# Attention probabilities of half of the blocks transposed in one TensorE run instead of two

## The chip, the cores and the metric

The kernel runs on one core of a Trainium2 chip. The core has five engines with their own instruction queues: PE (TensorE, the matrix engine, with its weight loads shown apart as PEld), ACT (ScalarE), DVE (VectorE), POOL (GpSimd) and SP (SyncE, which here issues the DMAs). The metric is the device time of one execution in microseconds (us); less is better. The kernel before takes 558.78 us, the median of three runs (558.47 to 558.86).

## The reference, cut to what matters

One encoder layer on a sequence of 512 tokens with 1024 channels, in float32. The normed and modulated input is projected to eight streams of 1024 channels; one branch is a gated recurrence, the other is attention over a grid of 8 rows by 64 columns, and both are projected, merged and normed.

```python
h = rms_norm(x, g_pre[l]) * (1.0 + scl[:, None, :]) + shift[:, None, :]
proj = h @ w_in[l]
xa, za, q, k, v, zb, ga, gb = jnp.split(proj, split_pts, axis=-1)
...
y_b = neighbourhood_attention(qh, kh, vh, rpb[l]) * jax.nn.silu(zb)
y_b = y_b @ w_pb[l]
merged = jax.nn.sigmoid(ga) * y_a + jax.nn.sigmoid(gb) * y_b
x = x + gate[:, None, :] * (merged @ w_o[l])
```

In the attention each of 16 heads lets a query see all 8 rows and a window of 16 columns around its own, with a learned bias per offset and a softmax over the 128 keys:

```python
s = jnp.einsum('bqhd,bwqkhd->bhqwk', q_r, k_win).astype(jnp.float32) * scale
s = s + jnp.transpose(bias, (0, 2, 1, 3)).astype(jnp.float32)[None]
p = jax.nn.softmax(s.reshape(B, H, GRID_W, win_r * WIN_C), axis=-1)
...
return jnp.einsum('bhqwk,bwqkhd->bqhd', p, v_win)
```

## The kernel before, in words

Every float32 product is made of three matmuls of rounded parts (high times high, high times low, low times high), so each operand is split: ACT writes the rounded high part (`whi`, line 380), and DVE or POOL subtracts it for the low part (`wlo`, line 383). A projection (`proj`) takes one 512 KB weight tile and runs 24 matmuls of 128x512 into one PSUM bank named `acc` (three matmuls for each of eight pieces of the contraction, line 386). Some 70 of these projections make up most of the program.

Attention is worked on in four groups of two head pairs. For each group the six projections for q, k and the output gate z come first, then PE computes the scores of both pairs in one piece (`sp`, 48 matmuls). The 64 columns of the grid are cut into four blocks of 16 columns; a block of 128 queries (8 rows by 16 columns) meets 24 or 32 key columns in 8 rows, so 192 keys at the edges (blocks 0 and 3) and 256 inside (blocks 1 and 2). `attend` runs `half` twice for a pair: for the edge blocks and for the inner ones. A half has two tiles of probabilities, each 128 queries by 384 or 512 numbers. For each tile:

- DVE adds the bias to the scores and takes the minimum (`ttr`, line 829); ACT takes the exponential (`exp`, line 836);
- PE transposes the tile in pieces of 128x128 into a bank of class `pt` (`ptr`, line 843): 3 pieces for an edge tile, 4 for an inner one;
- ACT copies the bank rounded to SBUF (`ph`, line 849) and DVE writes the rest beside it (`pl`, line 851), both into a tile `pp`;
- PE multiplies `pp` with the values (`pv`, 4 matmuls of 128x256).

ACT and DVE then put both results of a half together (`ev0`, line 868; `ev1` and `ev2`, lines 871 and 874). After both halves of a pair the sums of the softmax are inverted, go through DRAM to be spread over partitions, and come back as `rcx`; DVE multiplies the gate with them (`szr`, line 899) and then with the attention's result (`yb`, line 901). Both read two operands in SBUF. The tanh part of the next gate is `zt` on ACT (line 882) and `sz` on DVE (line 883).

There are 8 PSUM banks, and a class may hold only so many of them: `LIMITS` gives `pt` two, `pv` two, `acc` three. What runs when is not written by hand: each operation is given to a planner (`Plan`) with an engine, a cost in us and a rank, and the planner commits operations in the order of their ranks as far as their data, an engine and a buffer are free by its own reckoning. Its result is a fixed order of instructions on each engine. The matmuls of projections have ranks that let them fill every place where PE would otherwise wait for an attention step, so the attention's steps lie scattered between them. When an engine reaches an instruction whose inputs aren't there, all that stands behind it on that engine waits too.

Of the kernel before, what the change touches and what calls it, by code (L numbers as in the profile page):

```python
# [334 lines left out]
def layer(ctx, tc, x, x_t, par, w_m, w_v, w_in, w_blk, rpb, amask, w_pa, w_pb, w_o, g_final, out):  # L335
# [8 lines left out]
    def op(eng, cost, fn, rank, name="", **kw):  # L344
        return pl.op(eng, cost, fn, HEAD.get(name, rank), name=name, **kw)
# [18 lines left out]
    def B(cls):  # L364
        return pl.tile(cls, lambda i: ps.tile([P, 512], F32, tag=f"b{i}", name=nm(cls)))
# [31 lines left out]
    def const(name, shape, dt=F32):  # L397
        return pl.fixed(cp.tile(shape, dt, name=name))

    ident, onesc = const("ident", [P, P]), const("onesc", [P, P])  # L400
# [15 lines left out]
       r=[par_sb, ident], w=[pp0])  # L416
# [60 lines left out]
    for i in range(2):  # L477
        st, qs = B("hd"), []
        for j in range(4):
# [4 lines left out]
               r=[xTp[j, i]], w=[q], name=f"sq{i}{j}")  # L484
            if j:
                op(("DVE", "POOL"), (dve(512), pool_(512)), lambda e, a=qs[0], q=q: ENGINE[e].tensor_tensor(a.ap, a.ap, q.ap, op=ALU.add),
                   rank, r=[q], rw=[qs[0]], lock=True, name=f"sqa{i}{j}")
# [28 lines left out]
    for i in range(2):  # L516
        op("ACT", act(256), cast(lambda i=i: rbs.ap[:, 256 * i:256 * i + 256], lambda i=i: rb[i].ap[:, :256]), -1 + 0.4 * i,
           r=[rb[i]], w=[rbs.part()], name=f"rbs{i}")
# [286 lines left out]
    def attend(pr, sps, z, nbt, pos, pos0):  # L805
        sm, yt = C("sm", 8), T("yt")
        off = (pr % 2) * 256

        def half(bs):
            sp = sps[bs[0]]  # L810
            rt = pos0 + 0.1 * bs[0] - 0.2
            spv = lambda h, e: sp[h].ap.rearrange("p (e f) -> p e f", e=2)[:, e, :]
            rk = pos + 0.2 * bs[0]
            nk = nkb[bs[0]]
            edge = bs[0] == 0
            pv = [B("pv"), B("pv")]
            mn = C("mn", 4, 8)

            groups = [[(b, h) for b in bs] for h in range(2)] if edge else [[(b, h) for h in range(2)] for b in bs]
            for members in groups:  # L820
                pt_ = T("p")
                pv2 = lambda i, pt_=pt_: pt_.ap[:, i * nk:(i + 1) * nk]
                for i, (b, h) in enumerate(members):
                    def f(e_, i=i, b=b, h=h, pv2=pv2):
                        v = lambda a: a.rearrange("p (r c) -> p r c", r=ROWS)
                        e = bs.index(b)
                        nb = nbt[(1, 0, 0, 2)[b]].ap.rearrange("p (h f) -> p h f", h=2)
                        o = pv2(i).rearrange("p (c r) -> p r c", r=ROWS)
                        nc.vector.tensor_tensor_reduce(out=o, in0=v(spv(h, e)[:, :nk]), in1=v(nb[:, h, :nk]),  # L829
                                                       scale=1.0, scalar=3e38, op0=ALU.add, op1=ALU.min,  # L830
                                                       accum_out=mn.ap[:, 2 * e + h:2 * e + h + 1])
                    op("DVE", dve(nk) + 0.07, f, rt, r=[sp[h], nbt[(1, 0, 0, 2)[b]]], w=[pt_, mn], name="ttr")
                for i, (b, h) in enumerate(members):
                    def f(e_, i=i, b=b, h=h, pv2=pv2):
                        c = 2 * bs.index(b) + h
                        nc.scalar.activation(pv2(i), pv2(i), AF.Exp, bias=mn.ap[:, c:c + 1], scale=-1.0,  # L836
                                             accum_out=sm.ap[:, 4 * h + b:4 * h + b + 1])
                    op("ACT", act(nk, 1, True), f, rk - 0.25, r=[mn, pt_], w=[pt_, sm], name="exp")
                ptp, nt = B("pt"), nk // 64

                def f(e_, pt_=pt_, ptp=ptp, nt=nt):
                    for j in range(nt):
                        nc.tensor.transpose(ptp.ap[:, j * P:(j + 1) * P], pt_.ap[:, j * P:(j + 1) * P], ident.ap)  # L843
                op("PE", 0.03 + 0.11 * nt, f, rk - 0.3, r=[pt_, ident], w=[ptp], name="ptr")

                pp = W("pp", F32R)
                ppv = lambda pp=pp, nt=nt: pp.ap[:, :nt * 256].rearrange("p (j s q) -> p j s q", j=nt, s=2)
                pv4 = lambda ptp=ptp, nt=nt: ptp.ap[:, :nt * P].rearrange("p (j q) -> p j q", j=nt)
                op("ACT", act(nt * P), lambda e_, ppv=ppv, pv4=pv4: nc.scalar.copy(ppv()[:, :, 0, :], pv4()),  # L849
                   rk - 0.35, r=[ptp], w=[pp], name="ph")  # L850
                op("DVE", dve(nt * P), lambda e_, ppv=ppv, pv4=pv4: nc.vector.tensor_tensor(  # L851
                    ppv()[:, :, 1, :], pv4(), ppv()[:, :, 0, :].bitcast(F32), op=ALU.subtract),
                   rk - 0.35, r=[ptp], rw=[pp], name="pl")

                def f(e_, members=members, ppv=ppv):
                    for i, (b, h) in enumerate(members):
                        e = bs.index(b)
                        for j in range(2):
                            mm(pv[h].ap[:, e * 256:(e + 1) * 256], vt[pr // 2, b, j].ap[:, off + h * P:off + (h + 1) * P],
                               ppv()[:, (i if edge else 2 * i) + j].rearrange("p s q -> p (s q)"), j == 0, j == 1)  # L860
                op("PE", 0.49, f, rk - 0.4, r=[pp] + [vt[pr // 2, b, j] for b in dict(members) for j in range(2)],
                   w=[pv[h] for h in dict((h, b) for b, h in members)], name="pv")

            vp = T("vp")
            p3 = lambda t: t.ap.rearrange("p (e s q) -> p e s q", e=2, s=2)
            v3 = lambda: vp.ap[:, :256].rearrange("p (e q) -> p e q", e=2)
            for h in range(2):
                op("ACT", act(256), lambda e_, h=h: nc.scalar.copy(v3()[H[h]], p3(pv[h])[H[1 - h], :, 0, :]), rk - 0.45,
                   r=[pv[h]], w=[vp], name="ev0")
            for h in range(2):  # L870
                op("DVE", dve(256), lambda e_, h=h: nc.vector.tensor_tensor(v3()[H[h]], p3(pv[h])[H[h], :, 1, :], v3()[H[h]],
                   op=ALU.add), rk - 0.45, r=[pv[h], vp], w=[vp], name="ev1")
            for h in range(2):
                op("DVE", dve(256), lambda e_, h=h: nc.vector.tensor_tensor(
                    yt.ap[H[h]].rearrange("p (b q) -> p b q", b=4)[:, bs[0]:bs[1] + 1:bs[1] - bs[0]], p3(pv[h])[H[h], :, 0, :], v3()[H[h]],
                    op=ALU.add), rk - 0.45, r=[pv[h], vp], w=[yt], name="ev2")
        half((0, 3))
        half((1, 2))

        nz, oz = z  # L880
        sz, rc = T("sz"), rcs[pr % 2]
        op("ACT", act(512), lambda e: nc.scalar.activation(sz.ap, oz.ap, AF.Tanh, scale=0.5), nz - 1.9, r=[oz], w=[sz], name="zt")
        op("DVE", dve(512), lambda e: nc.vector.scalar_tensor_tensor(sz.ap, sz.ap, 1.0, oz.ap, op0=ALU.add, op1=ALU.mult),
           nz - 1.9, r=[oz], rw=[sz], name="sz")

        def recip(e):
            nc.vector.tensor_scalar(rc.ap[:, :8], sm.ap, 2.0, None, op0=ALU.mult)
            nc.vector.reciprocal(rc.ap[:, :8], rc.ap[:, :8])
            nc.vector.transpose(rct.ap[:, :32], rc.ap)


        rct, rcx = T("rct"), T("rcx")
        scr = pl.fixed(dp.tile([32, P], F32, name=f"rscr{pr}"))
        op("DVE", 0.5, recip, pos - 0.3, r=[sm], w=[rc, rct], lock=True, name="rc")
        op("SP", 0.5, lambda e: nc.sync.dma_start(turned(scr.ap), rct.ap[:, :32]), pos - 3, r=[rct], w=[scr], size=16384, late=SLACK, name="rcs")
        for h in range(2):
            src = bass.AP(scr.ap.tensor, scr.ap.offset + h * 512, [[0, 64], [1, 512]])
            load(rcx, lambda h=h: rcx.ap[H[h], :], src, pos - 3, 131072, r=[scr], name="rcl", late=1.0)
        op("DVE", dve(512), lambda e: nc.vector.tensor_tensor(rbc(sz.ap), rbc(sz.ap), nat(rcx.ap), op=ALU.mult),
           pos - 0.3, r=[rcx], rw=[sz], lock=True, name="szr")  # L900
        op("DVE", dve(512), lambda e: nc.vector.tensor_tensor(rbc(sz.ap), nat(yt.ap), rbc(sz.ap), op=ALU.mult), pos + 0.5, r=[yt],
           rw=[sz], lock=True, name="yb")
        ybh[pr], ybl[pr] = two("ybhl")
        op("ACT", act(512), cast(whole(ybh[pr]), whole(sz)), pos + 0.6, r=[sz], w=[ybh[pr]], name="ybh")
        op("DVE", dve(512), sub(whole(ybl[pr]), whole(sz), whole(ybh[pr])), pos + 0.6, r=[sz, ybh[pr]], w=[ybl[pr]], lock=True,
           name="ybl")
# [187 lines left out]
    for k in range(KD):  # L1094
        t, r = W("wc"), gcol.part()
# [51 lines left out]
    for k in range(KD):  # L1147
# [3 lines left out]
        for n in range(2):  # L1151
            v = lambda n=n, raw=raw: raw.ap[:, n * 512:(n + 1) * 512]
            op("DVE", dve(512), lambda e, n=n, v=v: nc.vector.tensor_tensor(v(), v(), gate[n].ap, op=ALU.mult), rank,
               r=[gate[n]], rw=[raw], lock=True, name="wog")
# [165 lines left out]
```

## Time and profile before

| | before |
|---|---|
| median of the runs | 558.78 us (558.47 to 558.86) |
| the profiled execution | 558.32 us |
| its span, first to last instruction | 556.5 us |
| mean granted TensorE clock | 0.996 |
| PE busy | 548.2 us (99%), 2769 matmuls |
| PEld busy | 457.3 us (82%) |
| DVE busy | 395.2 us (71%) |
| ACT busy | 320.6 us (58%) |
| POOL busy | 103.1 us (19%) |

The span is what the trace covers; the execution's own time has 1.8 us around it. The ends of matmuls are modelled and overlap with the next one, so a busy PE says only that a matmul was always in flight. The chain of waits goes back from the last instruction, at each step to what released it; its pieces in a row tell how long PE spent on each piece of work. The timeline shows instructions with their start and length, and idle time ahead of them with what ended it.

### The profile page before, as it was taken

The numbers are of one execution on the slowest core, as the hardware profiler recorded it, in microseconds if no ns is written. First come the engines' busy times: TensorE is split into PE (matmuls) and PEld (weight loads), VectorE is DVE, ScalarE is ACT, GpSimd is POOL, SyncE is SP. The second block draws the span as 40 slices with busy tenths as digits, with TensorE's granted clock in tenths as the row PEclk, the third lists the DMA queues.
The fourth block names the chain that finished last, engine by engine and source line by source line (L and its number), as shares of the span: only waits on it lengthen the run. The fifth ranks groups of instructions, "written<-read, shape, count | busy, mean of one in ns | idle before, by whom it ended". The sixth has DMA issues, their size and how long they took to land.

```text
span 556.5 us, 7644 instructions
## 1 busy us (share of the span) xinstructions
PE 548.2 (99%) x2769; PEld 457.3 (82%) x2769; DVE 395.2 (71%) x707; ACT 320.6 (58%) x557; POOL 103.1 (19%) x98
## 2 busy tenths in 40 slices
PE   8999999999999999999999999999999999999995
PEld 8888888888888888887887888888788888888884
DVE  5998733786786886898449978867968973569423
ACT  6542524863763772775986984996697242223242
POOL 0102657646547430000000000000000000000220
PEclk9999999999999999999999999999999999999998
DMA  8992994851741753035245045132237522480002
GB/s 311 408 407 110 312 296 174 199 166 50 189 145 68 177 146 133 2 102 185 83 145 170 6 146 170 39 114 67 85 104 275 190 77 75 150 304 1 0 38 115
DMA packets 30825, 82.54 MB, mean 148 GB/s; under 512 B 4548, under 2 KB 5700, under 8 KB 30788
## 3 DMA queue, kind: packets, MB, share of 16 engines
q1 hardware_dynamic: 30500, 81.73, 44.4%
q8 instruction: 22, 0.36, 0.3%
q10 hardware_dynamic: 288, 0.33, 0.2%
q14 instruction: 15, 0.12, 0.1%
HBM read 75.60 MB, written 6.44 MB: 147 GB/s over the span
## 4 chain that ended last, share of the span: by engine, by line
PE 99%; DVE 0%; POOL 0%; issue 0%; ACT 0%; POOLq 0%
PE acc L386 79%; PE hx L386 8%; PE pv L386 3%; PE pt L843 2%; PE sp L386 2%; PE gt L386 2%; PE hx L504 1%; PE hx L437 0%; PE hd L551 0%; PE hd L496 0%; PE hd L513 0%; DVE yo L1205 0%; DVE yo L1173 0%; DVE xr L1177 0%; ACT sd L1195 0%
## 5 line engine op out<-in xcount | busy, mean ns | idle before, releaser
L386 PE MATMUL acc<-hhl,whi 128*128 128x512 f32 x784 | 244.6, 393 | 0.0
L386 PEld LDWEIGHTS acc<-hhl,whi 128*128 128x128 f32 x784 | 143.7, 188 | 27.2
L386 PE MATMUL acc<-hhl,wlo 128*128 128x512 f32 x392 | 152.8, 390 | 0.0
L386 PEld LDWEIGHTS acc<-hhl,wlo 128*128 128x128 f32 x392 | 73.6, 188 | 15.8
L380 ACT CAST whi<-wraw 128x1024 fp32r<-128x1024 f32 x72 | 74.3, 1044 | 4.9 <-DMA wraw<-in_w_in_dram 3.7
L1184 POOL TENSOR_TENSOR yo<-yo,gfin 128x512 f32<-128x512 f32 x6 | 8.2, 1360 | 337.1 <-ACT xr L1181 337.1
L383 POOL TENSOR_TENSOR wlo<-wraw,whi 128x1024 fp32r<-128x1024 f32 x23 | 56.4, 2459 | 63.2 <-ACT whi L380 26.4
L383 DVE TENSOR_TENSOR wlo<-wraw,whi 128x1024 fp32r<-128x1024 f32 x49 | 59.3, 1220 | 3.0 <-ACT whi L380 2.8
L386 PE MATMUL acc<-woh,mhl 128*128 128x512 f32 (+1 forms) x144 | 40.4, 365 | 0.0
L386 PE MATMUL acc<-yahl,whi 128*128 128x512 f32 x128 | 39.4, 389 | 0.0
L386 PE MATMUL acc<-ybhl,whi 128*128 128x512 f32 x128 | 39.4, 389 | 0.0
L738 POOL TENSOR_TENSOR nb<-msk,braw 128x192 f32<-128x192 f32 (+1 forms) x48 | 31.1, 682 | 28.5 <-DMA braw<-in_rpb_dram 28.5
L836 ACT ACTIVATE p<-p,mn 128x192 f32<-128x192 f32 (+1 forms) x64 | 30.5, 478 | 5.6 <-DVE mn L829 5.5
L386 PE MATMUL hx<-vh,hhl 128*128 128x512 f32 x112 | 33.5, 389 | 0.0
L1069 DVE SCALAR_TENSOR_TENSOR gm<-gm,acc 128x512 f32<-128x512 f32 x16 | 11.0, 687 | 31.2 <-PE acc L386 31.1
L829 DVE CUSTOM_DVE_ANT_0 p<-sp,nb 128x192 f32<-128x192 f32 (+1 forms) x64 | 31.8, 612 | 0.7 <-POOL nb L738 0.2
L386 PEld LDWEIGHTS acc<-woh,mhl 128*128 128x128 f32 x144 | 26.1, 189 | 4.4
L386 PEld LDWEIGHTS acc<-yahl,whi 128*128 128x128 f32 x128 | 24.0, 188 | 5.0
L386 PEld LDWEIGHTS acc<-ybhl,whi 128*128 128x128 f32 x128 | 24.0, 188 | 5.0
L386 PE MATMUL acc<-wol,mhl 128*128 128x512 f32 (+1 forms) x72 | 26.3, 365 | 0.0
L851 DVE TENSOR_TENSOR pp<-pt,pp 128x384 fp32r<-128x384 f32 (+1 forms) x32 | 19.6, 624 | 8.9 <-ACT pp L849 8.8
L1064 ACT ACTIVATE gm<-acc 128x512 f32<-128x512 f32 x16 | 9.6, 599 | 27.4 <-PE acc L386 27.2
(195 smaller groups left out, 967.3 us busy)
## 6 DMA issues: line engine op xcount, KB each, us to landing
wraw<-in_w_in_dram SPq DMA_DIRECT2D x56, 512.0 KB
wc<-in_w_m_dram SPq DMA_DIRECT2D x22, 512.0 KB
vt<-vscr SPq DMA_DIRECT2D x20, 256.0 KB
vscr<-va SPq DMA_DIRECT2D x8, 512.0 KB
wraw<-in_w_pb_dram SPq DMA_DIRECT2D x8, 512.0 KB
wraw<-in_w_pa_dram SPq DMA_DIRECT2D x8, 512.0 KB
wo<-in_w_o_dram SPq DMA_DIRECT2D x8, 512.0 KB
wv<-in_w_v_dram SPq DMA_DIRECT2D x7, 512.0 KB
```

Of the source, the lines that this page charges most:

```text
L380: return lambda e: nc.scalar.copy(o(), i()) if e == "ACT" else nc.vector.tensor_copy(o(), i())
L383: return lambda e: ENGINE[e].tensor_tensor(o(), a(), b().bitcast(F32), op=ALU.subtract)
L386: nc.tensor.matmul(o, a, b, start=first, stop=last)
L504: op("PE", 0.3, lambda e: nc.tensor.matmul(wb.ap[:, :P], onesc.ap, onesc.ap, start=True, stop=True), 5000 + j, r=[onesc], hold=[wb], until ...
L738: nc.gpsimd.tensor_tensor(o, mv, view, op=ALU.subtract)
L829: nc.vector.tensor_tensor_reduce(out=o, in0=v(spv(h, e)[:, :nk]), in1=v(nb[:, h, :nk]), scale=1.0, scalar=3e38, op0=ALU.add, op1=ALU.min, ...
L836: nc.scalar.activation(pv2(i), pv2(i), AF.Exp, bias=mn.ap[:, c:c + 1], scale=-1.0, accum_out=sm.ap[:, 4 * h + b:4 * h + b + 1])
L843: nc.tensor.transpose(ptp.ap[:, j * P:(j + 1) * P], pt_.ap[:, j * P:(j + 1) * P], ident.ap)
L851: op("DVE", dve(nt * P), lambda e_, ppv=ppv, pv4=pv4: nc.vector.tensor_tensor(ppv()[:, :, 1, :], pv4(), ppv()[:, :, 0, :].bitcast(F32), op ...
L1064: op("ACT", act(512), lambda e: nc.scalar.activation(t.ap, o.ap, AF.Tanh, scale=0.5), n - 1.9, r=[o], w=[t], name="gm")
L1069: op("DVE", dve(512), lambda e: nc.vector.scalar_tensor_tensor(t.ap, t.ap, 1.0, o.ap, op0=ALU.add, op1=ALU.mult), n - 1.9, r=[o], rw=[t], ...
L1184: op(("DVE", "POOL"), (dve(w), pool_(w)), lambda e: ENGINE[e].tensor_tensor(y(), y(), gfin[n].ap[:, gs], op=ALU.mult), rank + 0.1, r=[gfin ...
```

## The change

The two tiles of a half are transposed by one operation of PE instead of two. Both tiles' exponentials come first; then one run of 6 or 8 transposes writes both `pt` banks, one tile into each; then the rounding, the subtraction and the product with the values follow tile by tile as before. The number of transposes, their shapes and the banks are unchanged. For the planner the joint operation costs `0.09 + 0.22 * nt` where two cost `0.03 + 0.11 * nt` each, and it needs both tiles and both banks.

```diff
             groups = [[(b, h) for b in bs] for h in range(2)] if edge else [[(b, h) for h in range(2)] for b in bs]
+            pts = []
             for members in groups:
                 pt_ = T("p")
...
                     op("ACT", act(nk, 1, True), f, rk - 0.25, r=[mn, pt_], w=[pt_, sm], name="exp")
-                ptp, nt = B("pt"), nk // 64
-
-                def f(e_, pt_=pt_, ptp=ptp, nt=nt):
+                pts.append(pt_)
+
+            nt = nk // 64
+            ptps = [B("pt"), B("pt")]
+
+            def f(e_):
+                for pt_, ptp in zip(pts, ptps):
                     for j in range(nt):
                         nc.tensor.transpose(ptp.ap[:, j * P:(j + 1) * P], pt_.ap[:, j * P:(j + 1) * P], ident.ap)
-                op("PE", 0.03 + 0.11 * nt, f, rk - 0.3, r=[pt_, ident], w=[ptp], name="ptr")
+            op("PE", 0.09 + 0.22 * nt, f, rk - 0.3, r=pts + [ident], w=ptps, name="ptr")
+            for members, ptp in zip(groups, ptps):
```

The planner makes another order of it on every engine within the attention stretch. Two places, both at the inner half of the second pair of the first group, which is the last half of that group. On DVE, in the kernel before, from the last combining step of the edge half (`yt`, line 874) on; `pp_1305` is the second tile's `pl`, `sz_830` is the first pair's gate (line 899 is `szr`, line 901 `yb`), `sz_1316` is `sz` of the second pair:

```order
L874 TENSOR_TENSOR yt_1307<-pv_1281,vp_1267 64x2x128
L851 TENSOR_TENSOR pp_1305<-pt_1295,pp_1305 128x4x128
L883 SCALAR_TENSOR_TENSOR sz_1316<-sz_1316,acc_1210 128x512
L899 TENSOR_TENSOR sz_830<-sz_830,rcx_1273 128x512
L901 TENSOR_TENSOR sz_830<-yt_1147,sz_830 128x512
L871 TENSOR_TENSOR vp_1339<-pv_1319,vp_1339 64x256
```

The same place in the changed kernel (its lines are 6 higher from line 843 on); `pp_1299` and `pp_1306` are the two tiles' `pl`, and lines 905, 907 and 889 are `szr`, `yb` and `sz`:

```order
L880 TENSOR_TENSOR yt_1301<-pv_1276,vp_1281 64x2x128
L857 TENSOR_TENSOR pp_1299<-pt_1283,pp_1299 128x4x128
L905 TENSOR_TENSOR sz_830<-sz_830,rcx_1255 128x512
L907 TENSOR_TENSOR sz_830<-yt_1141,sz_830 128x512
L889 SCALAR_TENSOR_TENSOR sz_1322<-sz_1322,acc_1216 128x512
L857 TENSOR_TENSOR pp_1306<-pt_1284,pp_1306 128x4x128
L383 TENSOR_TENSOR ybhl_1337<-sz_830,ybhl_1337 128x512
```

The last tile's `pl` stood ahead of `sz`, `szr` and `yb`; now it stands behind all three, with the first tile's `pl` ahead of them. The second and the third group have the same two pieces under other numbers.

On ACT at the same place, before; `vp` is `ev0` of the edge half, `pp_1305` the second tile's `ph`, `whi_1325` the rounding of a weight tile, whose subtraction POOL makes:

```order
L868 COPY vp_1267<-pv_1281 64x256
L849 CAST pp_1305<-pt_1295 128x4x128
L882 ACTIVATE sz_1316<-acc_1210 128x512
L380 CAST whi_1325<-wraw_1157 128x1024
L868 COPY vp_1339<-pv_1319 64x256
```

And in the changed kernel, with both tiles' `ph`:

```order
L874 COPY vp_1281<-pv_1276 64x256
L855 CAST pp_1299<-pt_1283 128x4x128
L855 CAST pp_1306<-pt_1284 128x4x128
L380 CAST whi_1316<-wraw_1143 128x1024
L888 ACTIVATE sz_1322<-acc_1216 128x512
```

The weight's rounding moved ahead of the gate's tanh, and both tiles' `ph` stand in a row. On PE the piece of the group between the scores and the last `pv` had transposes eight times, and has them four times; the matmuls between them are the same ones, in longer pieces. At its end the changed order is: 8 matmuls `pv`, 8 transposes, 12 matmuls of projections, 4 `pv` of `pp_1299`, 12 matmuls of projections, 4 `pv` of `pp_1306`.

## Rows read from the trace of the kernel before

**Rows 1.** The page: busy time and share of the span of PE, DVE, ACT and POOL; then the chain that ended last, by engine.

```profile
PE 548.2 (99%) x2769; PEld 457.3 (82%) x2769; DVE 395.2 (71%) x707; ACT 320.6 (58%) x557; POOL 103.1 (19%) x98
...
PE 99%; DVE 0%; POOL 0%; issue 0%; ACT 0%; POOLq 0%
```

**Rows 2.** The waits of PE in the whole span: who was waited for, us in total, times, longest.

```profile
PE hx L504 <- POOL epsc L452: 1.5, 1, 1.5
```

**Rows 3.** The chain of waits in order of time, within the attention stretch: start in us, length in us, what, how many instructions. `acc` are matmuls of projections, 128x512.

```profile
97.41 2.77 PE acc L386 x12
...
115.91 0.47 PE pv L386 x4
116.39 0.70 PE acc L386 x3
117.08 0.44 PE pt L843 x4
117.52 1.40 PE acc L386 x6
118.92 0.47 PE pv L386 x4
119.39 0.69 PE acc L386 x3
120.07 0.47 PE pv L386 x4
120.55 14.99 PE acc L386 x66
...
140.43 2.75 PE acc L386 x12
...
202.40 0.70 PE acc L386 x3
```

**Rows 4.** All instructions of the transposes' line: count, shortest, median and longest in ns, first and last start.

```profile
L843 PEld LDWEIGHTS pt<-ident,p x112: 138/140/144, 96.7 to 248.2; 128*128 128x128 f32 x112
L843 PE MATMUL pt<-ident,p x112: 270/272/273, 96.9 to 248.3; 128*128 128x128 f32 x112
```

**Rows 5.** The timeline of ACT at the end of the first group, and two copies `ph` and a weight's rounding close to each other in the fourth: start, length, what, idle time before and what ended it.

```profile
116.42 0.36 ACT L868 COPY vp<-pv 64x256 f32<-64x256 f32 x1 [1.04 <-PE pv L386]
117.61 0.59 ACT L849 CAST pp<-pt 128x512 fp32r<-128x512 f32 x1 [0.83 <-PE pt L843]
118.31 0.60 ACT L882 ACTIVATE sz<-acc 128x512 f32<-128x512 f32 x1
118.81 1.04 ACT L380 CAST whi<-wraw 128x1024 fp32r<-128x1024 f32 x1
...
248.60 0.59 ACT L849 CAST pp<-pt 128x512 fp32r<-128x512 f32 x1
249.08 1.05 ACT L380 CAST whi<-wraw 128x1024 fp32r<-128x1024 f32 x1
```

**Rows 6.** The timeline of DVE at the end of the first group, and two `pl` in a row in the fourth.

```profile
116.82 0.43 DVE L871 TENSOR_TENSOR vp<-pv,vp 64x256 f32<-64x256 f32 x1 [0.45 <-ACT vp L868]
117.28 0.88 DVE L874 TENSOR_TENSOR yt<-pv,vp 64x256 f32<-64x256 f32 x2
118.23 0.69 DVE L851 TENSOR_TENSOR pp<-pt,pp 128x512 fp32r<-128x512 f32 x1
118.95 0.69 DVE L883 SCALAR_TENSOR_TENSOR sz<-sz,acc 128x512 f32<-128x512 f32 x1
119.55 0.69 DVE L899 TENSOR_TENSOR sz<-sz,rcx 128x512 f32<-128x512 f32 x1
120.27 2.77 DVE L901 TENSOR_TENSOR sz<-yt,sz 128x512 f32<-128x512 f32 x1
122.97 0.86 DVE L871 TENSOR_TENSOR vp<-pv,vp 64x256 f32<-64x256 f32 x2
...
252.06 1.29 DVE L851 TENSOR_TENSOR pp<-pt,pp 128x512 fp32r<-128x512 f32 x2
```

**Rows 7.** The timeline of POOL around the same place.

```profile
113.14 2.41 POOL L383 TENSOR_TENSOR wlo<-wraw,whi 128x1024 fp32r<-128x1024 f32 x1 [1.27 <-ACT whi L380]
119.92 2.56 POOL L383 TENSOR_TENSOR wlo<-wraw,whi 128x1024 fp32r<-128x1024 f32 x1 [4.38 <-ACT whi L380]
```

**Rows 8.** The timeline of DVE at the same place of the third group, and the last rows of POOL's timeline between 190 and 265 us.

```profile
204.20 0.69 DVE L851 TENSOR_TENSOR pp<-pt,pp 128x512 fp32r<-128x512 f32 x1
204.91 0.69 DVE L883 SCALAR_TENSOR_TENSOR sz<-sz,acc 128x512 f32<-128x512 f32 x1
205.52 0.69 DVE L899 TENSOR_TENSOR sz<-sz,rcx 128x512 f32<-128x512 f32 x1
206.24 0.69 DVE L901 TENSOR_TENSOR sz<-yt,sz 128x512 f32<-128x512 f32 x1
...
199.15 2.40 POOL L383 TENSOR_TENSOR wlo<-wraw,whi 128x1024 fp32r<-128x1024 f32 x1 [1.26 <-ACT whi L380]
```

**Rows 9.** The timeline of PEld at the last `pv` of the first group: when its weights were loaded.

```profile
119.69 0.65 PEld L386 LDWEIGHTS pv<-pp,vt 128*128 128x128 f32 x4
```

**Rows 10.** A wait of PE early in the program: the timeline of DVE, of PEld and of PE.

```profile
25.87 1.23 DVE L383 TENSOR_TENSOR vl<-wv,vh 128x1024 fp32r<-128x1024 f32 x1 [0.23 <-ACT vh L380]
...
27.15 0.19 PEld L386 LDWEIGHTS hx<-vl,hhl 128*128 128x128 f32 x1 [0.28 <-DVE vl L383]
...
26.22 1.07 PE L386 MATMUL hx<-vh,hhl 128*128 128x512 f32 x4
27.15 0.50 PE L386 MATMUL hx<-vl,hhl 128*128 128x512 f32 x1
27.49 0.39 PE L386 MATMUL hx<-vh,hhl 128*128 128x512 f32 x1
```

## The prediction, made before the changed kernel ran

> **What bounds the kernel now.** I read the page's busy shares first, then PE's waits, then the chain of waits, and last the timelines of the four engines around the transposes. PE is busy for 99% of the span and the chain that ends last is 99% PE [rows 1]. PE waited once in the whole program, 1.5 us at its very start [rows 2]. So nothing is to be had by shortening a way through ACT or DVE: the time changes only if PE gets less to do, if the same work runs closer, or if a wait appears on PE where there is none. Such a wait can't be made good later, since PE has no idle place that would take it up.
>
> **What the change takes from PE.** All 112 transposes stay, with the same shapes [rows 4]. They follow each other at 0.44 us for 4 [rows 3], or 0.11 each, and a run of 8 should be two of these, 0.87. What goes is boundaries. From the scores to the last `pv` of a group the projections' matmuls lie in 13 pieces before and in 7 after (first three groups; 10 and 9 in the fourth): 19 pieces fewer in all. What is a boundary worth? In the undisturbed piece 66 matmuls take 14.99 us, 0.2271 each [rows 3]. Against that, 12 matmuls should take 2.725 and took 2.75 and 2.77; 6 should take 1.363 and took 1.40; 3 should take 0.681 and took 0.69 and 0.70. So a piece loses 0.01 to 0.045 us, the short ones, which are most of those that go, 0.01 to 0.02. I take 0.02: 19 x 0.02 = **0.4 us gained**, with 0.2 and 0.85 as the ends.
>
> **What it adds: a longer way from the transposes to `pv`.** Both tiles now pass ACT and DVE in a row. Take E as the end of a run of 8. The first tile's transposes end 0.44 before E, its `ph` takes 0.59 and the next ACT instruction starts 0.48 after it [rows 5], so the second `ph` ends about 0.67 after E, and with a free DVE the second `pl` (0.69) ends 1.4 after E [rows 6]. PE has 12 matmuls (2.75) and the first tile's `pv` (0.47) before it needs that [rows 3]; the weights of `pv` are loaded up to 0.38 ahead [rows 3, 9], which leaves 1.4 us. Behind the runs of 6 there are 9 to 18 matmuls and the way is shorter. In the changed order DVE is not always free by then: combining steps of the half before (0.86 and 0.88 [rows 6]) can stand ahead of `pl`, which pushes it back by up to 0.9 us, so that 0.5 us of room or more stays everywhere but at one place. Outside of that place I cost the longer way at nothing; the matmuls of the projections hide it.
>
> The one place is the end of a group. The last tile's `pl` now stands on DVE behind `szr`, `yb` and `sz`, where before it stood ahead of them. `yb` took 2.77 us there instead of 0.69 [rows 6, 8]. The rows show why: POOL's subtraction for a weight ran from 119.92 to 122.48 [rows 7], over `yb`, which ended 0.56 later; in the third group, where POOL has nothing after 201.55, `yb` took 0.69 [rows 8]. Before, nothing that PE needs soon stood behind `yb`. Now the last `pv` of the group does.
>
> Its working, from t0, the end of the edge half's last `pv` (116.39 in the old order [rows 3]):
>
> - PE: 8 transposes 0.87, 12 matmuls 2.75, 4 `pv` 0.47, 12 matmuls 2.75: the last `pv` is due at t0 + 6.84. Its weights load 0.38 ahead (119.69 for 120.07 [rows 3, 9]): t0 + 6.46.
> - ACT: `ev0` at 0.03 after t0 [rows 3, 5]; the first `ph` 0.03 after its transposes' end, t0 + 0.47; the second 0.48 later, 0.95; the weight's rounding 1.43 to 2.47 (1.04 long [rows 5]). POOL's instruction comes 0.07 after that (119.85 to 119.92 [rows 5, 7]): t0 + 2.54.
> - DVE: `ev1` at 0.43, `ev2` at 0.89, first `pl` at 1.80 (204.20 less 202.40 in the third group [rows 3, 8]), `szr` 0.61 later at 2.41, `yb` 0.72 after that, 3.13 (119.55 to 120.27 [rows 6]).
> - POOL is there at 2.54, between the two, as it was before (119.92 between 119.55 and 120.27). Then it went ahead of `yb` and ended 2.93 after `szr` began [rows 6, 7]: now t0 + 5.34. `yb` ends 0.56 later, the next DVE instruction starts 0.49 after POOL's end (122.97): `sz` at 5.83, the last `pl` 0.60 later at 6.43, its end at 7.12.
> - PE: in the early wait [rows 10] the weight load came 0.05 after DVE's end (27.10, 27.15). So 7.17, or 0.71 late. There the load was 0.24 late (its place was at 26.91, as the matmuls of that piece start 0.227 apart from 26.22) and PE lost 0.13: 27.49 where 26.90 + 2 x 0.227 = 27.36 was due. So 0.11 of lateness is free, and a group loses **0.6 us**.
>
> This holds for the first and the second group. In the third POOL has no such work: `yb` at 3.13, `sz` at 3.74, `pl` from 4.34 to 5.03, 1.4 us early. In the fourth the order is another one and POOL is idle [rows 8]; the last two `pl` come with over 0.5 us to spare. So 2 x 0.6 = **1.2 us lost**. The steps may be off by 0.15 each way per group; the ends are 0 (POOL comes after `yb`) and 0.8 (it comes before `szr`, below).
>
> **Sum.** The profiled execution took 558.32 us, a span of 556.5 and 1.8 around it; minus 0.4, plus 1.2, gives 559.1. It lies 0.46 under the median of the runs, so for the median 558.78 + 0.8 = **559.6 us**. That is 0.15% more; a measurement of this kernel can tell some 0.2%, here 1.1 us, from no change. The forecast is no change that can be told, with its own range 559.2 to 560.1.
>
> **Rivals.**
>
> *No wait at all.* If POOL's instruction is there only after `yb` has begun (t0 + 3.13, that is 0.6 later than I work out), `yb` takes 0.69 and the last `pl` ends at 5.03, as in the third group. For it: POOL's start hangs on a row of six ACT steps. Against it: 0.6 us is more than the few tenths by which such steps vary between the groups. What is left is the gain: 558.78 - 0.4 = 558.4.
>
> *POOL ahead of `szr`: slower.* The tanh of the gate stood ahead of the weight's rounding on ACT and now stands behind it, so POOL comes only 0.13 after `szr` instead of 0.37. If it comes 0.15 sooner than worked out, `szr` waits as well: POOL ends at 4.8, `szr` at 5.36, `yb` at 6.08, the last `pl` at 7.3, the load at 7.35, 0.89 late. That is 0.8 per group, 1.6 in all; minus 0.4, 560.0, just slower by the bound above, and 560.3 if the boundaries give 0.1 only. It decides at the point where the weight's rounding ends before t0 + 2.34. Rows show only the one direction, DVE held by POOL, and a slight stretch of POOL by `szr` (2.56 against 2.41 [rows 7]).
>
> The Trainium skill (SBUF — State Buffer, section Who interferes with whom) says that a DVE instruction with two SBUF inputs contends with a GpSimd instruction that reads SBUF, and that the order of issue, not the operation, decides who waits. The 2.77 against 0.69 us of `yb` agree. By that rule this rival is a matter of 0.13 us, and I leave it more than a remote chance.
>
> *Both banks held at once.* The run needs both `pt` banks, so it can begin only when the last `pl` of the half before has read its bank; before, one bank could be filled while the other was emptied. In this order the `pv` of that same `pl` stands ahead of the next run on PE, so the bank can't be the last thing waited for. But the same lateness would show at `pv`: with the 0.5 us that I find at the tightest of the other 14 places gone and 0.1 lost at each, 1.4 us come on top, 561.0. Against it: most places have 0.7 us or more.
>
> The Trainium skill (Perfetto Trace Analysis, section Matmuls) asks that independent groups rotate through banks so that the emptying of one overlaps the filling of the next, which speaks against this change. No row here shows PE waiting for a `pt` bank, and by the rule alone the time would be that of this rival.
>
> **Chances.** The forecast has 0.60: of it some 0.45 within the bound and 0.15 above it (over 559.9). No wait: 0.15, within the bound, with 0.04 of it faster, if the boundaries are worth more than the ends that I saw. POOL ahead of `szr`: 0.15, two thirds of it slower. Both banks: 0.10, nearly all of it slower. Together faster 0.04, within 0.2% 0.62, slower 0.34. The range for 8 times in 10 goes from the case without a wait, 558.2, to the case of POOL ahead of `szr` with half of its uncertainty, 560.5.
>
> **What would show it.** Right: PE has a wait of about 0.6 us at the last `pv` of the first and of the second group, released by DVE's `pl`, and none in the third; `yb` there takes near 2.8 us, with POOL's subtraction over it; the chain shows runs of 0.65 and 0.87 us for 6 and 8 transposes, and pieces of 12 matmuls at 2.74 to 2.77. Wrong: no wait on PE at all (then POOL came late), waits at other `pv` or at the transposes themselves (then the ways are longer than I worked out, or the banks count), or a run of 8 that isn't twice a run of 4. A time under 558.2 would mean that boundaries cost far more than the pieces show.

## The result, and the profile after

The changed kernel takes 561.06 us (median of five runs, 560.60 to 561.49), the kernel before 558.78 (558.47 to 559.18, now of five runs too): a ratio of 1.0037, 95% interval 1.0026 to 1.0048. It is slower by 0.4%, clear of the interval, and lies above the range of the prediction (558.2 to 560.5). The profiled execution took 561.49 us with a span of 559.5.

The page's busy shares (part 1) and the chain by engine (part 4), which answer to [rows 1]: PE has the same 2769 matmuls. The chain that ended last is followed back to 162.21 us only, so its 69% is nearly all of the stretch that it covers; what is new in it is DVE with 1%.

```profile
PE 548.9 (98%) x2769; PEld 458.7 (82%) x2769; DVE 397.1 (71%) x707; ACT 319.3 (57%) x557; POOL 102.3 (18%) x98
...
PE 69%; DVE 1%; issue 0%; ACT 0%
```

PE's waits over the whole span, beside [rows 2]: who was waited for, us in total, times, longest.

```profile
PE hx L504 <- POOL epsc L452: 1.5, 1, 1.5
PE pv L386 <- DVE pp L857: 1.4, 2, 0.7
PE hd L513 <- DVE rx L462: 0.8, 1, 0.8
```

The second line is new and is the one that was looked for: `pv` waits for `pl`, twice. The third is a wait of the start, where the two kernels have the same instructions and executions differ. DVE's row there in the changed kernel, and then in the kernel before, shows its cause:

```profile
14.85 1.24 DVE L462 SCALAR_TENSOR_TENSOR rx<-q,r 128x2 f32<-128x2 f32 x1
```

```profile
14.65 0.16 DVE L462 SCALAR_TENSOR_TENSOR rx<-q,r 128x2 f32<-128x2 f32 x1
```

In the changed kernel this small instruction began 0.03 us behind one of POOL's subtractions (14.82) and took 1.24 us; in the kernel before it began 0.04 us ahead of POOL (14.69) and took 0.16.

To size the second line: the view counts idle time only from a matmul's modelled end. By the ends of the single matmuls, the waiting `pv` ended 1.059 and 1.070 us after the matmul ahead of it where 0.115 is usual: **0.95 us lost each time**.

Where the time went shows best from marks on PE: the starts of the four pieces of scores, of the first gates behind them, and the end of the last matmul. Each group runs from one piece of scores to the next, the fourth to the gates (all in us).

| kernel | first scores | group 1 | group 2 | group 3 | group 4 | sum | gates to end |
|---|---|---|---|---|---|---|---|
| before | 92.43 | 43.03 | 43.01 | 43.01 | 37.55 | 166.60 | 290.67 |
| changed | 93.50 | 44.01 | 43.95 | 43.01 | 37.51 | 168.49 | 290.67 |

The first two groups are 0.98 and 0.94 longer, the others as long as before. That is 1.9 of the 2.28 us between the medians. In the two profiles the only other difference lies ahead of the first scores (93.50 against 92.43), where both kernels have the same instructions; where the remaining 0.4 of the medians lies, no profile of the median runs shows.

The chain in order of time (start, length, what; it is followed back to 162.21 us and no further) shows the second of the two waits, and the runs and pieces that answer to [rows 3]:

```profile
163.60 0.69 DVE pp L857
164.29 2.20 DVE sz L905
166.49 0.02 issue
166.52 0.69 DVE sz L907
167.21 0.60 DVE sz L889
167.81 0.61 DVE pp L857
168.42 0.14 issue
168.55 0.71 PE pv L386 x4
...
188.83 0.66 PE pt L848 x6
...
194.56 0.87 PE pt L848 x8
195.44 2.74 PE acc L386 x12
```

The end of the first group on DVE, beside [rows 6] (start, length, what):

```profile
115.30 2.17 DVE L893 TENSOR_SCALAR rc<-sm 128x8 f32<-128x8 f32 x1
...
117.87 0.83 DVE L877 TENSOR_TENSOR vp<-pv,vp 64x256 f32<-64x256 f32 x2
118.74 0.88 DVE L880 TENSOR_TENSOR yt<-pv,vp 64x256 f32<-64x256 f32 x2
119.64 0.69 DVE L857 TENSOR_TENSOR pp<-pt,pp 128x512 fp32r<-128x512 f32 x1
120.25 2.27 DVE L905 TENSOR_TENSOR sz<-sz,rcx 128x512 f32<-128x512 f32 x1
122.56 0.69 DVE L907 TENSOR_TENSOR sz<-yt,sz 128x512 f32<-128x512 f32 x1
...
123.77 0.69 DVE L857 TENSOR_TENSOR pp<-pt,pp 128x512 fp32r<-128x512 f32 x1
```

POOL there, beside [rows 7]:

```profile
115.05 2.39 POOL L383 TENSOR_TENSOR wlo<-wraw,whi 128x1024 fp32r<-128x1024 f32 x1 [2.60 <-ACT whi L380]
119.57 2.41 POOL L383 TENSOR_TENSOR wlo<-wraw,whi 128x1024 fp32r<-128x1024 f32 x1 [2.13 <-ACT whi L380]
```

And PE's last `pv` of that group, with the first piece behind the edge half's `pv` for the origin t0:

```profile
115.83 1.12 PE L386 MATMUL pv<-pp,vt 128*128 128x256 f32 x8
116.78 1.04 PE L848 MATMUL pt<-ident,p 128*128 128x128 f32 x8
...
124.60 0.71 PE L386 MATMUL pv<-pp,vt 128*128 128x256 f32 x4 [0.70 <-DVE pp L857]
```

POOL held DVE twice. Its first subtraction caught `rc`, the doubling of the softmax's sums: 128x8 numbers, 0.17 us when free, 2.17 here, released at POOL's end (115.05 + 2.39 = 117.44). Everything behind came late, so that `szr` was issued 0.7 us behind the start of POOL's second subtraction and was caught as well (2.27 instead of 0.69). `yb`, which I had expected to be caught, ran free.

In the third group `rc` was held too, but no second subtraction follows, and the last `pl` ended 0.87 us ahead of the start of its `pv` (211.64). So the first hold alone costs PE no more than 0.06 us there, at the first tile's `pv`. Beside [rows 8]:

```profile
203.22 2.17 DVE L893 TENSOR_SCALAR rc<-sm 128x8 f32<-128x8 f32 x1
...
208.17 0.68 DVE L905 TENSOR_TENSOR sz<-sz,rcx 128x512 f32<-128x512 f32 x1
...
210.09 0.68 DVE L857 TENSOR_TENSOR pp<-pt,pp 128x512 fp32r<-128x512 f32 x1
```

### The profile page after: what moved, and what is told of

It reads as the page before. It is cut to its first block, busy times and chain, and to the rows that moved or that the text cites. A ratio compares the mean times of both kernels' runs of the same rounds, so it can differ in the third digit from the quotient of the medians.

```text
span 559.5 us, 7637 instructions
## 1 busy us (share of the span) xinstructions
PE 548.9 (98%) x2769; PEld 458.7 (82%) x2769; DVE 397.1 (71%) x707; ACT 319.3 (57%) x557; POOL 102.3 (18%) x98
## 4 chain that ended last, share of the span: by engine, by line
PE 69%; DVE 1%; issue 0%; ACT 0%
PE acc L386 63%; PE gt L386 2%; PE pv L386 1%; PE pt L848 1%; PE sp L386 1%; DVE sz L905 0%; DVE pp L857 0%; DVE yt L880 0%; DVE yo L1211 0%; DVE sz L907 0%; DVE sz L889 0%; DVE yo L1179 0%; DVE vp L877 0%; DVE xr L1183 0%; ACT sd L1201 0%
## 5 line engine op out<-in xcount | busy, mean ns | idle before, releaser
L386 PEld LDWEIGHTS acc<-hhl,whi 128*128 128x128 f32 x784 | 145.5, 188 | 29.1
L981 DVE SCALAR_TENSOR_TENSOR xc<-acc,prm,xc 128x511 f32<-128x511 f32 (+1 forms) x24 | 18.0, 749 | 14.8 <-ACT xc L974 14.2
L386 PE MATMUL acc<-yahl,wlo 128*128 128x512 f32 x64 | 24.9, 390 | 0.0
```

The source lines that it names most:

```text
L386: nc.tensor.matmul(o, a, b, start=first, stop=last)
L981: nc.vector.scalar_tensor_tensor(a, b, wcol, a, op0=ALU.mult, op1=ALU.add)
```

## The experiments

Two theories were tried. **P**: POOL's work holds DVE at the end of a group, and the last `pl` stands behind what is held. **W**: the joint run itself makes the way from transposes to `pv` too long, or holds both banks too long, and POOL only happens to run there. All medians below are of 10 or 11 runs, against 559.03 to 559.08 us for the kernel before on the same chip, unless told otherwise.

| kernel | first scores | group 1 | group 2 | group 3 | group 4 | sum | median | ratio to before, 95% |
|---|---|---|---|---|---|---|---|---|
| rc_short | 94.74 | 43.55 | 43.57 | 42.95 | 37.51 | 167.58 | 560.36 | 1.0010 to 1.0027 |
| no_read | 93.10 | 43.00 | 42.95 | 43.03 | 37.51 | 166.49 | 559.22 | 0.9994 to 1.0011 |
| edge_only | 93.18 | 43.58 | 43.57 | 42.97 | 37.56 | 167.68 | 560.59 | 1.0016 to 1.0035 |
| inner_only | 94.05 | 42.97 | 42.95 | 42.95 | 37.56 | 166.44 | 559.32 | 0.9999 to 1.0017 |
| pl_first | 92.95 | 42.97 | 42.97 | 42.99 | 37.51 | 166.43 | 558.82 | 0.9986 to 1.0004 |
| pl_first_rc | 93.44 | 43.01 | 42.94 | 42.95 | 37.51 | 166.41 | 558.47 | 0.9983 to 1.0000 |
| no_read_2nd | 92.92 | 43.98 | 43.91 | 43.03 | 37.51 | 168.43 | 560.87 (one run) | |
| before_again | 93.42 | 43.02 | 43.02 | 43.01 | 37.55 | 166.60 | 559.22 | 0.9996 to 1.0013 |

From the gates to the end all ten profiles have 290.67 us.

**rc_short**: the inversion without the instruction that was held.

```diff
-            nc.vector.tensor_scalar(rc.ap[:, :8], sm.ap, 2.0, None, op0=ALU.mult)
-            nc.vector.reciprocal(rc.ap[:, :8], rc.ap[:, :8])
+            nc.vector.reciprocal(rc.ap[:, :8], sm.ap)
...
+        op("ACT", act(512), lambda e, h=ybh[pr]: nc.scalar.activation(h.ap, sz.ap, AF.Copy, scale=0.5), pos + 0.6, r=[sz], w=[ybh[pr]], name="ybh")
```

> The changed kernel, but the inversion of the sums starts with the reciprocal: its TENSOR_SCALAR (times 2) is gone, and the factor 0.5 is applied where the gate's product is rounded (both steps that exist anyway). The order of all other instructions is that of the changed kernel. Theory P (POOL's reads hold DVE, and the last `pl` of a group stands behind): the reciprocal isn't held (it took 0.20 us under POOL's subtraction in the kernel before), the first `pl` comes 1 us sooner, `szr` is issued ahead of POOL's second subtraction and takes 0.69, `yb` is held instead; the wait at the last `pv` falls from 0.95 to 0.4 to 0.7 in the first and second group, the 0.06 at the first tile's `pv` goes; 559.9 to 560.5 us. Rival W (the joint run of 8 makes the way from transposes to `pv` too long, POOL only happens to run there): the waits stay at 0.95, 561.0. A third outcome, that the reciprocal is held as the TENSOR_SCALAR was (2 us), leaves everything as in the changed kernel as well, and shows in its row.

DVE at the end of the first group, then POOL and PE there:

```profile
116.49 0.19 DVE L894 RECIPROCAL rc<-sm 128x8 f32<-128x8 f32 x1
...
119.94 0.69 DVE L857 TENSOR_TENSOR pp<-pt,pp 128x512 fp32r<-128x512 f32 x1
120.55 0.68 DVE L905 TENSOR_TENSOR sz<-sz,rcx 128x512 f32<-128x512 f32 x1
121.26 2.77 DVE L907 TENSOR_TENSOR sz<-yt,sz 128x512 f32<-128x512 f32 x1
...
124.56 0.68 DVE L857 TENSOR_TENSOR pp<-pt,pp 128x512 fp32r<-128x512 f32 x1
```

```profile
116.23 2.39 POOL L383 TENSOR_TENSOR wlo<-wraw,whi 128x1024 fp32r<-128x1024 f32 x1 [2.57 <-ACT whi L380]
120.77 2.72 POOL L383 TENSOR_TENSOR wlo<-wraw,whi 128x1024 fp32r<-128x1024 f32 x1 [2.14 <-ACT whi L380]
```

```profile
117.02 1.12 PE L386 MATMUL pv<-pp,vt 128*128 128x256 f32 x8
...
125.38 0.71 PE L386 MATMUL pv<-pp,vt 128*128 128x256 f32 x4 [0.36 <-DVE pp L857]
```

As P expected: the reciprocal starts 0.26 us into POOL's subtraction and isn't held, `szr` is ahead of the second subtraction, `yb` is held instead, and the waits are 0.61 us each (matmul ends 0.720 and 0.721 apart, less 0.115). W would have left them at 0.95.

**no_read**: four of POOL's subtractions become fills.

```diff
-        op(engs, costs, sub(whole(low), whole(raw), whole(hi)), n - 2.1, r=[raw, hi], w=[low], lock=True, name=f"wlo{n}")
+        op(engs, costs, (lambda e: nc.gpsimd.memset(low.ap.bitcast(F32), 0.0)) if n in (20, 21, 26, 27) else sub(whole(low), whole(raw), whole(hi)), n - 2.1, r=[raw, hi], w=[low], lock=True, name=f"wlo{n}")
```

> The changed kernel with four of POOL's subtractions (the two at the end of the first and of the second group) turned into a fill with zeros of the same tile: POOL reads nothing there. It leaves out the low parts of four weight tiles; the order on all engines is that of the changed kernel. Theory P: `rc` takes 0.17, `szr` and `yb` 0.69, the last `pl` is early, both waits of 0.95 go and the 0.06 of the first two groups too; 558.9 to 559.2 us. Rival W: the waits at the last `pv` stay (0.5 or more each), 560 to 561. If a fill holds DVE as a subtraction does, the rows of `rc` and `szr` show over 2 us still, and nothing is told apart.

The waits are gone, as P had it (559.22, just above its bounds; the 0.06 stays in the third group alone). But the reason is plainer than I had meant: a fill needs no input, so POOL ran both early and was idle at the place. POOL's timeline:

```profile
111.98 1.87 POOL L701 MEMSET wlo<- 128x1024 f32 x2
125.61 2.40 POOL L383 TENSOR_TENSOR wlo<-wraw,whi 128x1024 fp32r<-128x1024 f32 x1 [11.76 <-ACT whi L380]
```

So this shows that without POOL there the changed order costs nothing, not that reading is what holds DVE.

**edge_only** and **inner_only**: the joint run for one kind of half, the old code for the other (inner_only has `if not edge`).

```diff
+            if edge:
...
+                op("PE", 0.09 + 0.22 * nt, f, rk - 0.3, r=pts + [ident], w=ptps, name="ptr")
...
+            else:
...
+                    op("PE", 0.03 + 0.11 * nt, f, rk - 0.3, r=[pt_, ident], w=[ptp], name="ptr")
```

> Joint runs for the edge halves only; the inner halves have two operations as in the kernel before. The planner still puts the last `pl` of a group on DVE behind `szr`, `yb` and `sz`, and PE's order at the end of the group is as in the changed kernel (12 projection matmuls between the two `pv`). Theory P: the inner halves' joint runs are not needed for the loss: waits of 0.7 to 1.0 at the last `pv` of the first and second group, 560.6 to 561.2 us. Rival W: without the joint run of 8 the second tile's way is the old one and the waits are gone, 558.4 to 559.0.

> Joint runs for the inner halves only; the edge halves as in the kernel before. Here the planner puts both `pl` of the last half ahead of `sz`, `szr` and `yb`, and leaves only 3 projection matmuls between the two `pv`. Theory P: `rc` may be held as in the changed kernel, but nothing that PE needs soon stands behind `szr` and `yb`: waits of at most 0.1 to 0.3 in the first and second group, 558.6 to 559.3 us. Rival W: the joint run of 8 is here, and the last `pv` is wanted even sooner (3 matmuls after the first instead of 12), so the waits are there, 0.7 or more each, 560.3 or more.

This pair speaks most clearly against W. With edge_only the inner halves have their old two operations, and the waits are there; DVE in the first group:

```profile
114.48 0.16 DVE L940 TENSOR_SCALAR rc<-sm 128x8 f32<-128x8 f32 x1
...
119.03 0.68 DVE L952 TENSOR_TENSOR sz<-sz,rcx 128x512 f32<-128x512 f32 x1
119.74 2.78 DVE L954 TENSOR_TENSOR sz<-yt,sz 128x512 f32<-128x512 f32 x1
...
123.04 0.68 DVE L904 TENSOR_TENSOR pp<-pt,pp 128x512 fp32r<-128x512 f32 x1
```

They are 0.63 and 0.61 us, not the 0.7 to 1.0 that I expected, since here `rc` began 0.30 us ahead of POOL's subtraction (114.78) and was over before it: again only `yb` was held. With inner_only the joint run of 8 is there and both `pl` stand ahead of `szr`; DVE in the first group, then POOL:

```profile
116.00 0.16 DVE L940 TENSOR_SCALAR rc<-sm 128x8 f32<-128x8 f32 x1
...
121.22 1.90 DVE L952 TENSOR_TENSOR sz<-sz,rcx 128x512 f32<-128x512 f32 x1
```

```profile
116.01 2.40 POOL L383 TENSOR_TENSOR wlo<-wraw,whi 128x1024 fp32r<-128x1024 f32 x1 [2.93 <-ACT whi L380]
```

`szr` took 1.90 us, and PE has no wait in any group (559.32 us, just above what P expected). `rc` ran free here, 0.01 us ahead of POOL, so inner_only speaks against W but doesn't test the order of `pl` under both holds; pl_first does.

**pl_first**: the changed kernel, with both `pl` of the last half ahead of `szr`.

```diff
-AFTER = [('wc71', 'wc41')]
+AFTER = [('wc71', 'wc41')] + [(f"szr{p}", f"pl{p + 1}.2") for p in (0, 2)]
...
-           pos - 0.3, r=[rcx], rw=[sz], lock=True, name="szr")
+           pos - 0.3, r=[rcx], rw=[sz], lock=True, name=f"szr{pr}")
```

> The changed kernel with one rule more for the planner: in the first and second group `szr` (and with it `yb`) may only be placed once the last half's second `pl` is placed. On DVE both `pl` then stand ahead of `sz`, `szr` and `yb`; the planner also moves the last `pv` from 12 to 3 projection matmuls behind the first tile's. `rc` and POOL's subtractions stay as they are. Theory P: `rc` is still held for about 2.2 us, `szr` or `yb` too, but nothing waits for those two; the second `pl` ends 0.6 us after the first and the last `pv` doesn't wait; at most the 0.06 at the first tile's `pv` stays. The three first groups take 43.0 to 43.1 us each from scores to scores (the changed kernel 44.01, 43.95, 43.01), the run 559.0 to 559.4 us. Rival W, which the runs so far speak against: the last `pv` is wanted 2 us sooner and waits 0.7 or more; groups of 43.7 or more, 560.5 or more.

DVE at the end of the first group:

```profile
114.69 2.19 DVE L893 TENSOR_SCALAR rc<-sm 128x8 f32<-128x8 f32 x1
...
119.06 1.29 DVE L857 TENSOR_TENSOR pp<-pt,pp 128x512 fp32r<-128x512 f32 x2
120.26 0.68 DVE L889 SCALAR_TENSOR_TENSOR sz<-sz,acc 128x512 f32<-128x512 f32 x1
120.86 1.08 DVE L905 TENSOR_TENSOR sz<-sz,rcx 128x512 f32<-128x512 f32 x1
```

POOL still holds `rc` and `szr`, the last `pv` is wanted 2 us sooner than in the changed kernel, and it doesn't wait: only the 0.06 at the first tile's `pv` stays. The median, 558.82, is a little under what was expected; the groups are 42.97, 42.97 and 42.99.

**pl_first_rc**: both edits together.

> The rule of pl_first and the short inversion of rc_short together. Theory P: no wait in any group, also none of 0.06 at the first tile's `pv`; from the first scores to the gates 166.40 to 166.45 us (before: 166.60; the change without its waits is worth 0.18 there, by no_read). A gain of 0.15 to 0.2 us can't be told from the kernel before in the medians: ratio 0.999 to 1.001. Rival B (a boundary between pieces is worth 0.02 us, as the prediction had it): 166.2, a gain of 0.4.

166.41 us, as P had it, without any wait. It is 0.19 us less than before; Rival B's 0.4 isn't there. The ratio, 0.9983 to 1.0000, doesn't tell it from the kernel before.

**no_read_2nd**: the fill only in place of the second subtraction of each of the two groups (n in (21, 27)).

> As no_read, but only the second of POOL's two subtractions at the end of the first and of the second group is a fill with zeros (it leaves out the low parts of two weight tiles). Theory P: `rc` is held for 2.2 us as in the changed kernel and the 0.06 at the first tile's `pv` stays, but `szr` and `yb` take 0.69 each, the last `pl` ends 1.6 us sooner and the wait of 0.95 is gone altogether: groups of 43.05 us. Should the hold of `rc` alone be enough, a wait of 0.4 to 0.95 stays.

A miss that teaches. POOL ran the fill right behind the first subtraction, under `rc`:

```profile
114.50 2.39 POOL L383 TENSOR_TENSOR wlo<-wraw,whi 128x1024 fp32r<-128x1024 f32 x1 [2.60 <-ACT whi L380]
116.83 0.96 POOL L701 MEMSET wlo<- 128x1024 f32 x1
```

```profile
114.75 3.06 DVE L893 TENSOR_SCALAR rc<-sm 128x8 f32<-128x8 f32 x1
...
120.00 0.69 DVE L857 TENSOR_TENSOR pp<-pt,pp 128x512 fp32r<-128x512 f32 x1
```

`rc` was held for 3.06 us, 0.9 longer, through the subtraction and the fill. Now it is the first tile's `pl` that is late, and the first tile's `pv` waits 0.96 where it had waited 0.06; the last `pv` doesn't wait, as expected. So a longer hold of `rc` goes straight into PE's time. What the hold of 2.17 us alone costs, this run doesn't tell; the third group of the changed kernel does (0.06).

**before_again**: the kernel before with a line that does nothing.

> The kernel before with one line more that does nothing: the same instructions in the same order. It tells how far two medians of one program lie apart, and how far the start (to the first scores, 92.43 us in the profile of before and 93.1 to 94.7 in the five others, though the instructions up to there are the same) moves from execution to execution. If the start only scatters: 558.8 to 559.3 us, ratio within 0.999 to 1.001, groups of 43.0, 43.0, 43.0 and 37.55, and a first score at 92.4 to 94. If instead something in the changed kernels makes their start 0.3 us longer, this run shows its first scores below 92.8.

The groups come back to 0.01 us, and the start does not: 93.42 instead of 92.43. Over the ten profiles the first scores begin between 92.43 and 94.74. Where a median differs from what its groups give (by -0.4 to +0.5 us here), I put it down to this scatter of the start, which is not shown. One cause of it is seen in the changed kernel's profile, the `rx` that POOL held by chance; what moves the rest, no experiment looked into.

## Why the prediction was wrong

- *What bounds the kernel, and where a wait can cost*: right. PE bounds it, a wait on PE can't be made good, and the whole loss is at the last `pv` of the first and second group, released by `pl` behind POOL's hold of DVE. The third group loses 0.06, which its missing boundaries give back, and the fourth nothing.
- *The longer way costs nothing elsewhere; "Both banks held at once"*: the first is right, and that rival fell; its 561.0 is near the measured time by chance. No transposes wait anywhere, and no `pv` but those named, apart from 0.06 at the first tile's `pv` in the first three groups.
- *The runs*: 0.65 to 0.66 and 0.87 us for 6 and 8 transposes, as worked out.
- *"First `pl` at 1.80"*: **this is the step that failed.** I read it from the third group of before [rows 3, 8], where DVE was free at t0, and took that over. The sum has only the second of POOL's two subtractions. The first one [rows 7] ended 0.84 us ahead of t0 in the old order (115.55, 116.39); in the changed one it ended 0.49 behind it (117.44), and until then it held `rc`, which stands ahead of `ev1`. From t0 (115.83 + 1.12 = 116.95) the weight's rounding ended at +2.54 (predicted 2.47) and POOL began at +2.62 (2.54), but the first `pl` began at +2.69 instead of 1.80 and `szr` at +3.30 instead of 2.41. So "POOL ahead of `szr`" is what happened, 0.95 per group instead of the 0.6 of the forecast or the 0.8 of that rival, and by another way than that rival had: POOL wasn't early, DVE was late. Its point of decision was put on the wrong engine.
- The trace of before could have told me. There a TENSOR_SCALAR of 128x16 (line 916), also behind a start of POOL's, took 2.37 us at 63.94; and `rc` itself ran just ahead of POOL (105.89 against 106.08) or at its end (115.42, POOL ended 115.55). I looked at two-input instructions alone.
- *The rest of that sum* holds. Without the hold of `rc` (rc_short, t0 = 117.02 + 1.12 = 118.14) the first `pl` began at +1.80, `szr` at +2.41, POOL at +2.63, `yb` at +3.12 and the last `pl` at +6.42, against 1.80, 2.41, 2.54, 3.13 and 6.43; the wait was 0.61, where 0.6 was worked out.
- *0.4 us gained by fewer boundaries*: mis-sized. pl_first_rc has no waits and is 0.19 shorter than before, just under the lower end that I gave. The fourth group has 8 pieces after the change, not 9, so 20 boundaries go, and each is worth 0.01 on average. Why the short pieces of before seemed to lose more is not shown; they are rounded to 0.01 and their ends modelled.

The groups thus give 1.9 us where I had 0.8. They alone would have made 560.7, above the range too. The remaining 0.4 of the difference of the medians is put down to the start and not shown.

## What to carry to other kernels

When an order moves, follow every instruction ahead of the one that matters on its engine, the small ones too: 128x8 numbers held DVE for 2 us here because they were issued 0.25 us behind POOL's start. What an edit costs can sit in what a planner then puts elsewhere: with edge_only the inner halves' code was the old one and they lost 0.6 us each, and one rule on the order (pl_first) took the whole loss away. Where the start of a program scatters by more than the effect, compare marks inside the trace; they came back to 0.01 us.

## What the runs showed of the hardware

- POOL holds some DVE instructions and not others. TENSOR_SCALAR 128x8 went from 0.17 us to between 2.17 and 2.19 under a subtraction; RECIPROCAL of the same size took 0.19 and 0.20 under one, and `pl`, with one input in PSUM and one in SBUF, took 0.69 at 119.64 as it does when POOL is idle. The Trainium skill (SBUF — State Buffer, section Who interferes with whom) counts `tensor_scalar` among those that can take the ports shared with GpSimd; the 2.17 us agree. It exempts a GpSimd instruction that only writes for DVE instructions with two SBUF inputs, and not for these: the hold of 3.06 us, through a subtraction and the fill behind it, agrees.
- In these rows, who starts first goes first. `rc` 0.25 us behind POOL's start was held; 0.01 ahead of it (inner_only, in the first and the second group) it took 0.16 us while POOL worked on. `rx`, with two inputs in SBUF, took 1.24 us at 0.03 behind (changed kernel) and 0.16 at 0.04 ahead (before). In the other direction, a subtraction that began 0.22 us behind `szr` (rc_short) took 2.72 instead of 2.39 us.
